# Moving GpSimd's arithmetic to VectorE in a hybrid RWKV-7, attention and MoE block, with preparation inputs issued a unit ahead

## The chip, the cores and the metric

One core of a Trainium2 chip. The metric is the device time of one launch in microseconds; a lower one is better. All tensors are float32 in HBM. Products that need float32 accuracy are made of three matmuls on the high and low parts of their operands (`mm3`): high by high, high by low, low by high. So most operands are split first: ScalarE copies the high part (`split`, L92), another engine subtracts it from the original to get the low part (L93).

## What is computed

A sequence of 2048 tokens of width 1024 goes through one layer:

```python
h = rms_norm(x, norm_mix_g)
u = h @ w_in
u_rwkv = centred_token_shift(u[..., :RWKV_COLS], mu_prev, mu_next)
...
y_rwkv = rwkv7_bidir(u_rwkv, ...)        # 8 heads of 64, forward and backward
y_attn = banded_gqa_attention(q, k, v)   # window of 128, blocks of 128
merged = sigmoid(gl_rwkv) * (y_rwkv @ w_proj_rwkv) + sigmoid(gl_attn) * (y_attn @ w_proj_attn)
x = x + merged @ w_out
x = x + expert_choice_moe(rms_norm(x, norm_ffn_g), w_router, w_gate, w_up, w_down)
return rms_norm(x, norm_final_g)
```

In the RWKV part the keys are scaled by `k_k` and normalized per head, decays and learning rates come from low-rank inputs, and the state runs over the tokens in both directions. In the expert part each of 16 experts takes the 256 tokens with the highest affinity.

## The kernel before

The kernel runs in stages, one after the other.

*First product.* `RwkvIn` computes the 15 channel blocks of `u_rwkv` (L78 to L80) and shifts them over the tokens; they go to HBM as `us`. Weights come through `w_load`, whose low part is GpSimd's unless another engine is named.

*Preparation.* `token_mixers` runs 32 units: 8 blocks of 256 tokens by 4 pairs of heads (`Prep`). `front()` computes decays (`th`, scans L289 and L290), `G`, `kd`, `KB` and `PR`; `back()`, called while the next unit's `front()` has been issued, makes the chunk matrices `A` (L328, L331), the bonus `bg` and transposed keys. Chunks have 32 tokens. Once per block `lora_in` loads the low-rank inputs and the key blocks, squares the keys, sums them per head on TensorE (L217), takes the reciprocal root by a chain of operations on 16 columns (`rsqrt`, L106 to L108), and transposes the result `rn` (L224). Between a unit's steps `between` issues five matmuls of `Proj` (`gates`, L459): these compute q, k, v and the gates, 2112 matmuls in all, as filling for TensorE. From the ninth unit on it also issues one step of an inversion (`Invert`, L386 and L387): a multiply of GpSimd and a sum of VectorE, 31 steps for each of three matrices here.

*Steps.* The state's chain goes over 64 chunks in both directions (L615 to L640); VectorE's multiply L636 carries the state from one chunk to the next. Around the chain, in an order that the program fixes, lie the other gate matmuls, the five other inversions, attention (L698 to L753) and the normalization of the RWKV output (`finish_rwkv`, L653 to L673).

*Mixer output.* Projections, the gated sum (`gl`, L953), the residual, the router's softmax (L1003 to L1009).

*Routing.* `route` finds each expert's threshold bit by bit: 30 rounds of a count (L1048), a sum over partitions by TensorE (L1051), and two operations of one column (L1052, L1053). GpSimd meanwhile makes `r5` and the low parts of the first three experts' weights.

*Experts.* 16 experts in 8 slices each; GpSimd only issues gathers and scatters there.

Each engine executes its queue in the order of the program that a scheduler has laid out; DMAs are issued by SP, ScalarE's queue and GpSimd's. The order around the change is set by the code: `issue_after(mark)` puts the gates behind a given instruction. The main loop reads:

```python
                if n < len(todo):
                    t0, p = todo[n]
                    if p == 2 and n + 4 < len(todo):
                        t1 = todo[n + 4][0]
                        lora[t1] = lora_in(k, t1, NT)
                    pp.append(Prep(k, t0, p, lora[t0], between))
                    pp[n].load()
                    pp[n].front()
                if n:
                    pp[n - 1].back()
```

## Time and profile before

| what | value |
|---|---|
| median of three runs | 3549.74 us (3541.02 to 3562.28) |
| the profiled execution | 3546.9 us, span 3545.0 us, mean granted clock of TensorE 0.944 |
| busy: TensorE, VectorE, ScalarE, GpSimd | 3201.6, 2288.4, 1447.1, 1018.3 us |
| stages (from 0): first product, transition, preparation | to 365, 400, 1035 us |
| steps, mixer output, routing, experts | to 1888, 2322, 2391, 3545 us |
| GpSimd in the experts | 180.0 us, gathers and scatters |

The stages are cut by the time of their first and last instructions. Between 1035 and 1052 us the last unit's matrices travel to the chain. A busy share is the time in which an engine executes, whatever slows it; an engine that waits for another counts as idle.

### The profile page before, as it was taken

The numbers are of one execution on the slowest core, as the hardware profiler recorded it, in microseconds if no ns is written. First come the engines' busy times: TensorE is split into PE (matmuls) and PEld (weight loads), VectorE is DVE, ScalarE is ACT, GpSimd is POOL, SyncE is SP. The second block draws the span as 40 slices with busy tenths as digits, with TensorE's granted clock in tenths as the row PEclk, the third lists the DMA queues.
The fourth block names the chain that finished last, engine by engine and source line by source line (L and its number), as shares of the span: only waits on it lengthen the run. The fifth ranks groups of instructions, "written<-read, shape, count | busy, mean of one in ns | idle before, by whom it ended". The sixth has DMA issues, their size and how long they took to land. (4 is left out here: it accounts for less than half of the span.)

```text
span 3545.0 us, 65905 instructions
## 1 busy us (share of the span) xinstructions
PE 3201.6 (90%) x26062; PEld 2620.6 (74%) x26062; DVE 2288.4 (65%) x4469; ACT 1447.1 (41%) x2679; POOL 1018.3 (29%) x1023
## 2 busy tenths in 40 slices
PE   7999687788778999899997999939999999999998
PEld 6888576666656556566665888829999999999997
DVE  7433467776777867976666555565666666666664
ACT  4111354544433444544543333214444444444443
POOL 3110245465743323233333222230211121112111
PEclk9999798899888999999998999959999999999999
DMA  4222576767678666667855555344766676667663
GB/s 145 92 75 86 158 208 178 212 193 205 180 215 203 160 151 165 183 164 194 199 152 198 196 196 189 137 171 157 258 238 224 227 257 241 221 227 258 240 221 132
DMA packets 464579, 665.19 MB, mean 188 GB/s; under 512 B 162312, under 2 KB 345480, under 8 KB 445968
## 3 DMA queue, kind: packets, MB, share of 16 engines
q1 hardware_dynamic: 387824, 535.14, 49.2%
q10 hardware_dynamic: 58304, 59.79, 5.3%
q0 software_dynamic: 18144, 66.07, 4.9%
q8 instruction: 205, 3.36, 0.4%
q14 instruction: 102, 0.84, 0.1%
HBM read 483.66 MB, written 177.21 MB: 186 GB/s over the span
## 5 line engine op out<-in xcount | busy, mean ns | idle before, releaser
L459 PE MATMUL mm<-h,w 128*128 128x512 f32 x2112 | 624.9, 429 | 18.8 <-ACT h L92 4.2
L86 PE MATMUL pg<-xs,wg 128*128 128x256 f32 x2048 | 583.8, 285 | 0.0
L87 PE MATMUL pg<-xs,wg 128*128 128x256 f32 x2048 | 582.5, 284 | 0.0
L88 PE MATMUL pg<-xs,wg 128*128 128x256 f32 x2048 | 580.0, 283 | 0.0
L459 PEld LDWEIGHTS mm<-h,w 128*128 128x128 f32 x2112 | 392.5, 199 | 116.5 <-issue 11.0
L87 PEld LDWEIGHTS pg<-xs,wg 128*128 128x128 f32 x2048 | 392.8, 192 | 4.6 <-DVE xs L1158 0.2
L86 PEld LDWEIGHTS pg<-xs,wg 128*128 128x128 f32 x2048 | 392.5, 192 | 4.6 <-ACT xs L1157 0.2
L88 PEld LDWEIGHTS pg<-xs,wg 128*128 128x128 f32 x2048 | 392.8, 192 | 0.0
L93 DVE TENSOR_TENSOR wg<-raw,wg 128x2048 fp32r<-128x2048 f32 x125 | 286.2, 2290 | 106.3 <-ACT wg L92 106.1
L93 POOL TENSOR_TENSOR w<-wraw,w 128x1024 fp32r<-128x1024 f32 x86 | 210.1, 2444 | 295.0 <-ACT w L92 251.7
L92 ACT ACTIVATE w<-wraw 128x1024 fp32r<-128x1024 f32 x135 | 142.5, 1057 | 273.3 <-issue 159.7
L92 ACT ACTIVATE wg<-raw 128x2048 fp32r<-128x2048 f32 x128 | 244.2, 1908 | 6.0 <-DMA raw<-w_exp 6.0
L1221 ACT ACTIVATE sg<-pg 128x256 f32<-128x256 f32 x128 | 49.3, 385 | 480.6 <-PE pg L88 458.6
L1147 POOL DMA_INDIRECT x<-z,idx x30 | 33.5, 1117 | 597.9 <-DVE z L1183 545.2
L627 ACT ACTIVATE W<-ps 32x128 f32<-32x128 f32 x512 | 137.2, 268 | 162.5 <-PE ps L622 145.6
L87 PE MATMUL py<-wd,hd 128*128 128x512 f32 x512 | 203.1, 397 | 0.0
L78 PE MATMUL mm<-h,w 128*128 128x512 f32 x480 | 188.9, 395 | 14.7 <-ACT w L92 12.2
L86 PE MATMUL py<-wd,hd 128*128 128x512 f32 x512 | 201.0, 393 | 0.0
L88 PE MATMUL py<-wd,hd 128*128 128x512 f32 x512 | 198.4, 390 | 0.0
L79 PE MATMUL mm<-h,w 128*128 128x512 f32 x480 | 188.6, 394 | 0.7 <-DVE h L126 0.7
L80 PE MATMUL mm<-h,w 128*128 128x512 f32 x480 | 188.2, 393 | 0.3 <-POOL w L93 0.3
L1222 DVE TENSOR_TENSOR sg<-pg,sg 128x256 f32<-128x256 f32 x128 | 54.0, 422 | 194.7 <-ACT sg L1221 194.7
(305 smaller groups left out, 7108.6 us busy)
## 6 DMA issues: line engine op xcount, KB each, us to landing
raw<-w_exp SPq DMA_DIRECT2D x128, 1536.0 KB, 6.9
wraw<-w_in SPq DMA_DIRECT2D x103, 512.0 KB, 4.5
PRA<-pra SPq DMA_DIRECT2D x64, 512.0 KB, 5.4
pra<-PR SPq DMA_DIRECT2D x64, 256.0 KB, 3.8
pra<-A SPq DMA_DIRECT2D x64, 256.0 KB, 3.7
kt<-KT ACTq DMA_DIRECT2D x128, 128.0 KB, 4.4
...
KT<-kt SPq DMA_DIRECT2D x128, 128.0 KB, 4.4
```

The costliest lines, as they stand in the source:

```text
L78: nc.tensor.matmul(ps, lhsT=w[:, 0, i], rhs=hs[i][:, 0], start=(i == 0), stop=False)
L79: nc.tensor.matmul(ps, lhsT=w[:, 0, i], rhs=hs[i][:, 1], start=False, stop=False)
L80: nc.tensor.matmul(ps, lhsT=w[:, 1, i], rhs=hs[i][:, 0], start=False, stop=(i == KD - 1))
L86: nc.tensor.matmul(out, lhsT=w[0], rhs=x[0], start=start, stop=False)
L87: nc.tensor.matmul(out, lhsT=w[0], rhs=x[1], start=False, stop=False)
L88: return nc.tensor.matmul(out, lhsT=w[1], rhs=x[0], start=False, stop=stop)
L92: nc.scalar.activation(hi, x, AF.Copy)
L93: (eng or nc.vector).tensor_sub(lo, x, hi)
L459: nc.tensor.matmul(self.ps, lhsT=w[:, t // 2, i], rhs=h[:, t % 2], start=(self.i == 0), stop=(self.i == 3 * KD - 1))
L627: nc.scalar.activation(W[qd(u), o, e].rearrange("p g i -> p (g i)"), ps[qd(u), 128:256], AF.Copy)
L1221: nc.scalar.activation(sg, pg[:, 0], AF.Silu)
L1222: nc.vector.tensor_mul(sg, pg[:, 1], sg)
```

## The change

GpSimd keeps its memsets, the copies of the identity that the chain needs, and indirect DMAs; its rows fall from 772 to 221 in the program. All other work is VectorE's or ScalarE's, or is left out. In the preparation, `PR` is made in four operations of 256 columns that read `G` from a buffer with one more column of ones per chunk, so the copies at the edges disappear. ScalarE takes the copies `gc`, the squares of the first stage, and the scale and bias of `yt`. `lora_in` becomes the class `LoraIn`, whose loads, products and norms are spread over the units of the block before; `krv` is loaded a unit ahead; the stores of `PR` stand at the start of `back()`. `Proj` loads raw weights ahead of their split, and 72 gate matmuls, not 24, stand at the beginning of the preparation. Of the 2112 gate matmuls 1178 stood ahead of the chain's first matmul and 1240 stand there now; the rest lie in the steps. In the routing, constants are loaded before the mixer output, and the low parts of the first three experts' weights are made by VectorE in 36 pieces of 256 columns, one for each bit where there are some left.

```diff
-BUFS = dict(all=3, th=2, ta=2, vt4=1, kk=2, A=2, KT=2, bg=2, krv=3, kd=2)
+BUFS = dict(all=3, th=2, ta=2, vt4=1, kk=2, A=2, KT=2, bg=2, kd=2, KB=2)
...
-    split(nc, w[:, 0], w[:, 1], raw, eng or nc.gpsimd)
+    split(nc, w[:, 0], w[:, 1], raw, eng)
...
-            if i % 2:
-                nc.gpsimd.tensor_mul(sq, x, x)
-            else:
-                nc.scalar.activation(sq, x, AF.Square)
...
+class LoraIn:
...
-            nc.gpsimd.tensor_sub(t[64:], raw[64:], t[64:])
...
+            nc.vector.tensor_sub(t[64:], raw[64:], t[64:])
...
+    def keys(self):
+        k, nc = self.k, self.k.nc
+        self.sq = []
+        for p in range(NPAIR):
+            sq = k.prep.tile([128, self.N], F32, name="sq", bufs=NPAIR)
+            nc.sync.dma_start(sq, k.us[:, 3 + 3 * p, self.sl])
+            self.sq.append(sq)
+
+    def squares(self):
+        for p in range(NPAIR):
+            self.k.nc.scalar.activation(self.sq[p], self.sq[p], AF.Square, scale=self.k.v("k_k", p))
+
+    def norms(self):
+        k, nc = self.k, self.k.nc
+        NJ = self.N // 128
+        ps = k.ps_l.tile([128, NJ, NPAIR, 2], F32, name="pl")
+        for p in range(NPAIR):
+            for j in range(NJ):
+                nc.tensor.matmul(ps[:, j, p], lhsT=self.sq[p][:, j * 128:(j + 1) * 128], rhs=k.bones2, start=True,
+                                 stop=True)
+        ss = k.prep.tile([128, 8 * NJ], F32, name="ss")
+        nc.vector.tensor_scalar(ss, ps.rearrange("p j q e -> p (j q e)"), 1e-24, None, op0=ALU.max)
+        self.rn = k.prep.tile([128, 8 * NJ], F32, name="rn", bufs=2)
+        rsqrt(k, k.prep, self.rn, ss)
+
+    def rows(self):
+        k, nc = self.k, self.k.nc
+        pt = k.ps_l.tile([8, self.N], F32, name="pl")
+        for j in range(self.N // 128):
+            nc.tensor.transpose(pt[:, j * 128:(j + 1) * 128], self.rn[:, j * 8:j * 8 + 8], k.ident)
+        self.rt = k.rts[self.t0 // self.N % 2]
+        nc.vector.tensor_copy(self.rt[0:8], pt)
...
-        G = tile("G", (2, NT))
-        nc.scalar.activation(G, th, AF.Exp, scale=-0.5 * DECAY)
+        G = k.G[self.t0 // NT * NPAIR + p & 1]
+        nc.scalar.activation(G[:, 0, :, 1:], cv(th)[:, 0], AF.Exp, scale=-0.5 * DECAY)
+        nc.scalar.activation(G[:, 1, :, :C], cv(th)[:, 1], AF.Exp, scale=-0.5 * DECAY)
...
-        nc.gpsimd.tensor_mul(kd, kd, both(kt))
+        nc.vector.tensor_mul(kd, kd, both(kt))
...
-        nc.gpsimd.tensor_mul(PR[:, :, :, 1], both(rt).rearrange("p d (c t) -> p d c t", t=C), cv(G))
...
-        ck, cG = kk.rearrange("p (c t) -> p c t", t=C), cv(G)
-        nc.vector.tensor_mul(PR[:, 0, :, 0, 1:], ck[:, :, 1:], cG[:, 0, :, :C - 1])
-        nc.vector.tensor_mul(PR[:, 1, :, 0, :C - 1], ck[:, :, :C - 1], cG[:, 1, :, 1:])
-        nc.gpsimd.tensor_copy(PR[:, 0, :, 0, 0:1], ck[:, :, 0:1])
-        nc.gpsimd.tensor_copy(PR[:, 1, :, 0, C - 1:], ck[:, :, C - 1:])
-        nc.gpsimd.tensor_copy(k.gc[:, 0, p, c0:c0 + NC], cG[:, 0, :, C - 1])
+        for d in range(2):
+            for x, t in ((0, kk), (1, rt)):
+                g0 = x if d == 0 else 1 - x
+                nc.vector.tensor_mul(PR[:, d, :, x], t.rearrange("p (c t) -> p c t", t=C), G[:, d, :, g0:g0 + C])
+        nc.scalar.activation(k.gc[:, 0, p, c0:c0 + NC], G[:, 0, :, C], AF.Copy)
...
-        nc.gpsimd.tensor_copy(k.gc[:, 1, p, lo:lo + NC][:, ::-1], cG[:, 1, :, 0])
-        for e in range(2):
-            nc.sync.dma_start(k.pra[self.q][half(e), :, p, e, self.ul].rearrange("r d c x -> r d (c x)"),
-                              PR[half(e)].rearrange("p d c x t -> p d (c x t)"))
+        nc.scalar.activation(k.gc[:, 1, p, lo:lo + NC][:, ::-1], G[:, 1, :, 0], AF.Copy)
...
+        for e in range(2):
+            nc.sync.dma_start(k.pra[self.q][half(e), :, p, e, self.ul].rearrange("r d c x -> r d (c x)"),
+                              PR[half(e)].rearrange("p d c x t -> p d (c x t)"))
...
-        nc.gpsimd.tensor_add(kd[:, 0], kd[:, 0], kd[:, 1])
-        nc.gpsimd.tensor_mul(kd[:, 1], rt, kd[:, 0])
+        nc.vector.tensor_add(kd[:, 0], kd[:, 0], kd[:, 1])
+        nc.vector.tensor_mul(kd[:, 1], rt, kd[:, 0])
...
-        nc.scalar.activation(bg[:, 0], bg[:, 0], AF.Identity, bias=k.v("ln_b", p))
...
-            (eng or nc.vector).tensor_mul(tmp[:, :i, :i], X[:, r, r], col[:, None, :].to_broadcast([128, i, i]))
+            nc.vector.tensor_mul(tmp[:, :i, :i], X[:, r, r], col[:, None, :].to_broadcast([128, i, i]))
...
+        for _ in range(2):
+            self.load()
...
+        n = self.loaded
+        if n < len(self.todo) + self.done:
+            k = self.k
+            raw = k.wpool.tile([128, KD, 128], F32, name="wraw", bufs=k.raw_bufs)
+            k.nc.sync.dma_start(raw, k.I["w_in"][self.order[n]])
+            self.raw.append(raw)
+            self.loaded += 1
+
+    def split(self):
+        if self.raw:
+            k = self.k
+            raw = self.raw.pop(0)
+            w = k.wpool.tile([128, 2, KD, 128], F32R, name="w")
+            split(k.nc, w[:, 0], w[:, 1], raw)
+            self.w.append(w)
...
-                    while len(self.w) < 2 and len(self.w) < len(self.todo):
-                        self.load()
+                    while len(self.w) < 2 and self.raw:
+                        self.split()
+                        if not self.done:
+                            self.load()
...
+                if self.i == KD and self.done:
+                    self.load()
...
-        nc.vector.scalar_tensor_tensor(out=yt[:, p].rearrange("c (k t) -> c k t", t=C), in0=pt[:, p],
-                                       scalar=k.v("ln_w", p), in1=bg[:, p, 0].rearrange("c (k t) -> c k t", t=C),
-                                       op0=ALU.mult, op1=ALU.add)
-    nc.gpsimd.tensor_mul(yt, yt, bg[:, :, 1])
+        nc.scalar.activation(yt[:, p].rearrange("c (k t) -> c k t", t=C), pt[:, p], AF.Identity,
+                             scale=k.v("ln_w", p), bias=k.v("ln_b", p))
+    nc.vector.tensor_add(yt, yt, bg[:, :, 0])
+    nc.vector.tensor_mul(yt, yt, bg[:, :, 1])
...
-    nc.gpsimd.tensor_sub(qs[64:], qr[64:], qs[64:])
+    nc.vector.tensor_sub(qs[64:], qr[64:], qs[64:])
...
-    nc.gpsimd.tensor_sub(kl[:, :, :W], kr[:, :, :W], kh[:, :, :W])
+    nc.vector.tensor_sub(kl[:, :, :W], kr[:, :, :W], kh[:, :, :W])
...
+            lora = {0: LoraIn(k, 0, NT)}
+            for i in range(3):
+                lora[0].load(i)
+            lora[0].keys()
...
+                    inv.run(1)
+
+            gates.run(GATE_FIRST)
+            ln = lora[0]
+            ln.squares()
+            ln.norms()
+            for i in range(3):
+                ln.make(i)
+            gates.run(GATE_FIRST)
+            ln.rows()
...
+                p = n % NPAIR
...
+                    t0 = todo[n][0]
+                    if n == 0:
+                        pp.append(Prep(k, t0, 0, lora[t0], between))
+                        pp[0].load()
+                    if n + NPAIR - p < len(todo):
+                        t1 = todo[n + NPAIR - p][0]
+                        if p == 0:
+                            lora[t1] = LoraIn(k, t1, NT)
+                        ln = lora[t1]
+                    else:
+                        ln = None
+                    if n + 1 < len(todo) and p < NPAIR - 1:
+                        pp.append(Prep(k, t0, p + 1, lora[t0], between))
+                        pp[n + 1].load()
+                    if ln:
+                        if p == 0:
+                            ln.load(1)
+                            ln.load(2)
+                        elif p == 1:
+                            ln.make(1)
+                            ln.keys()
+                            ln.load(0)
+                        elif p == 2:
+                            ln.make(2)
+                            ln.squares()
                     pp[n].front()
                 if n:
                     pp[n - 1].back()
+                if n < len(todo) and ln:
+                    if p == 2:
+                        ln.norms()
+                        ln.make(0)
+                    elif p == 3:
+                        ln.rows()
+                        pp.append(Prep(k, t1, 0, ln, between))
+                        pp[n + 1].load()
...
-        gates.eng = nc.gpsimd
...
-                nc.gpsimd.tensor_add(gl[:, 0], gl[:, 0], gl[:, 1])
+                nc.vector.tensor_add(gl[:, 0], gl[:, 0], gl[:, 1])
...
-                nc.vector.scalar_tensor_tensor(out=z, in0=x, scalar=rs, in1=gz, op0=ALU.mult, op1=ALU.mult)
+                with tc.issue_after(last):
+                    nc.vector.scalar_tensor_tensor(out=z, in0=x, scalar=rs, in1=gz, op0=ALU.mult, op1=ALU.mult)
...
+def route_constants(k, pool):
...
+    k.rc = [ld("same_e", 128), ld("less_e", 128), ld("rmask", 256), ld("iota", CAP + NBLK + 1)]
+    k.rc.append(pool.tile([128, 128], BF16, name="same_b"))
+    nc.vector.tensor_copy(k.rc[4], k.rc[0])
+    k.iota = pool.tile([128, CAP], BF16, name="iota_b")
+    nc.vector.tensor_copy(k.iota, k.rc[3][:, :CAP])
...
+        def part(a, i):
+            nc.vector.tensor_sub(rem, a, r5[:, :, :, i])
+            nc.scalar.activation(r5[:, :, :, i + 1], rem, AF.Copy)
+
+        rest = {27: lambda: part(k.aff, 2), 24: lambda: part(rem, 3)}
...
+            count = nc.vector.tensor_scalar(junk, aTf, cand.bitcast(F32)[:, 0:1], None, op0=ALU.is_ge, op1=ALU.add,
+                                            accum_out=cnt)
+            with tc.issue_after(count.ins):
+                if bit in rest:
+                    rest[bit]()
+                else:
+                    next(small, 0)
...
+        def first(raw):
+
+            wg = ws.tile([128, 2, 2, KD, 128], F32R, name="wg")
+            wd = ws.tile([128, 2, KD * 128], F32R, name="wd")
+            lo = []
+            for t, r in ((wg.rearrange("p s a i c -> p s (a i c)"), raw[:, 0:2].rearrange("p a i c -> p (a i c)")),
+                         (wd, raw[:, 2].rearrange("p a b -> p (a b)"))):
+                nc.scalar.activation(t[:, 0], r, AF.Copy)
+                lo += [(t, r, slice(j, j + 256)) for j in range(0, r.shape[1], 256)]
+            return (wg, wd), lo
+
+        def pieces(todo):
+            for t, r, sl in todo:
+                nc.vector.tensor_sub(t[:, 1, sl], r[:, sl], t[:, 0, sl])
+                yield 1
+
...
-            w = [weights(raws.pop(0), nc.gpsimd) for _ in range(3)]
+            w, lo = zip(*(first(raws.pop(0)) for _ in range(3)))
...
+        small = pieces([x for t in lo for x in t])
+        route(k, rp, small)
```

TensorE at the beginning of the preparation (`mm` are gates, `sq` squared keys, `rn` the norms, `lora,wup` the first unit's product), before:

```order
L459 MATMUL mm<-h,w 128x512 x24
L217 MATMUL pl<-bones_134,sq 128x2 x2
L279 MATMUL pt<-ident,krv 128x128 x2
L217 MATMUL pl<-bones_134,sq 128x2 x6
L224 MATMUL pl<-ident,rn 8x128 x2
L265 MATMUL pl<-lora_2387,wup 128x256
```

and now:

```order
L495 MATMUL mm<-h,w 128x512 x48
L469 MATMUL pt<-ident,ev 128x128 x4
L495 MATMUL mm<-h,w 128x512 x24
L235 MATMUL pl<-bones_134,sq 128x2 x8
L300 MATMUL pt<-ident,krv 128x128 x4
L246 MATMUL pl<-ident,rn 8x128 x2
L286 MATMUL pl<-lora_2490,wup 128x256
```

There are 72 gates where 24 stood, and the sums of squares and the transposition of `rn` follow them.

TensorE around the second block's norms, before:

```order
L217 MATMUL pl<-bones_134,sq 128x2 x2
L348 MATMUL pt<-ident,KB 128x128 x4
L459 MATMUL mm<-h,w 128x512
L217 MATMUL pl<-bones_134,sq 128x2 x2
L459 MATMUL mm<-h,w 128x512 x4
L279 MATMUL pt<-ident,krv 128x128 x2
L224 MATMUL pl<-ident,rn 8x128 x2
L265 MATMUL pl<-lora_2387,wup 128x256
```

In the changed order the sums stand here,

```order
L495 MATMUL mm<-h,w 128x512 x5
L367 MATMUL pt<-ident,KB 128x128 x4
L495 MATMUL mm<-h,w 128x512 x5
L235 MATMUL pl<-bones_134,sq 128x2 x8
L286 MATMUL pl<-lora_2490,wup 128x256
```

and the transposition of `rn` here, 27 rows further on:

```order
L495 MATMUL mm<-h,w 128x512 x5
L367 MATMUL pt<-ident,KB 128x128 x4
L495 MATMUL mm<-h,w 128x512 x5
L246 MATMUL pl<-ident,rn 8x128 x2
L286 MATMUL pl<-lora_2654,wup 128x256
```

A unit's matmuls and gates lie between them now; the transposition was right behind the sums and a handful of gates.

VectorE at the start of the routing (`aff` the affinities, `aT` their transposition, `junk` the count, `wg,wd` experts' weights), before:

```order
L995 SCALAR_TENSOR_TENSOR z<-x_22686,rs_22761,gz 128x1024
L1008 RECIPROCAL sms<-sms 128x1
L1009 TENSOR_SCALAR aff<-sme,sms 128x16
L1038 COPY aT<-pr 128x256
L1048 TENSOR_SCALAR junk,cnt<-aT,cand 128x256
L1052 TENSOR_SCALAR mi<-pr 128x1
L1053 SCALAR_TENSOR_TENSOR cand<-mi,cand 128x1
L1048 TENSOR_SCALAR junk,cnt<-aT,cand 128x256
L1052 TENSOR_SCALAR mi<-pr 128x1
```

and now:

```order
L1090 TENSOR_SCALAR aff<-sme,sms 128x16
L1076 SCALAR_TENSOR_TENSOR z<-x_22657,rs_22732,gz 128x1024
L1294 TENSOR_TENSOR wg<-raw,wg 128x256 x4
L1294 TENSOR_TENSOR wd<-raw,wd 128x256 x4
L1123 COPY aT<-pr 128x256
L1129 MEMSET cand 128x1
L1142 TENSOR_SCALAR junk,cnt<-aT,cand 128x256
L1294 TENSOR_TENSOR wg<-raw,wg 128x256
L1151 TENSOR_SCALAR mi<-pr 128x1
L1152 SCALAR_TENSOR_TENSOR cand<-mi,cand 128x1
L1142 TENSOR_SCALAR junk,cnt<-aT,cand 128x256
```

`z` stands behind `aff`; eight pieces of weights stand ahead of the loop and one in each round behind the count.

## Rows read from the trace of the kernel before

**Rows 1.** Stage, its us; busy us of PE, PEld, DVE, ACT, POOL; clock; DMA.
```profile
0.00:365.00 365.00, 345.39 (x1519) 285.00 (x1520) 178.88 (x215) 82.04 (x84) 63.71 (x67) 0.99 0.29 98
365.00:400.00 35.00, 7.06 (x29) 5.67 (x27) 13.22 (x26) 9.31 (x19) 7.81 (x9) 0.58 0.62 187
400.00:537.00 137.00, 121.33 (x958) 99.77 (x958) 87.33 (x138) 70.71 (x135) 57.38 (x69) 0.91 0.69 195
537.00:1035.00 498.00, 397.19 (x3142) 315.48 (x3140) 349.83 (x514) 228.38 (x442) 280.18 (x304) 0.89 0.68 198
...
1052.00:1888.00 836.00, 765.83 (x9966) 500.39 (x9966) 625.03 (x1493) 386.90 (x1138) 266.78 (x350) 0.94 0.68 171
1888.00:2322.00 434.00, 403.41 (x1926) 333.33 (x1927) 243.66 (x511) 141.42 (x216) 125.23 (x69) 0.97 0.55 188
2322.00:2391.00 69.00, 13.60 (x84) 9.31 (x85) 48.84 (x165) 10.15 (x9) 28.35 (x15) 0.50 0.47 172
```

**Rows 2.** What TensorE waited for in the preparation: total us, times, longest.
```profile
PE pl L224 <- DVE rn L108: 37.3, 8, 8.9
PE pt L328 <- DVE KB L303: 17.8, 7, 4.1
```

**Rows 3.** Groups of the preparation: busy us, mean ns | idle before, releasers.
```profile
L386 POOL TENSOR_TENSOR tmp<-X,N 128x1 f32<-128x1 f32 (+30 forms) x93 | 109.1, 1173 | 57.0 <-DVE X L387 30.5 <-DMA N<-pra 11.2 <-DVE rsq_t L107 8.3
...
L93 DVE TENSOR_TENSOR w<-wraw,w 128x1024 fp32r<-128x1024 f32 x46 | 72.3, 1574 | 28.1 <-ACT w L92 28.0
L296 POOL TENSOR_TENSOR kd<-kd,krv 128x512 f32<-128x512 f32 x32 | 49.8, 1558 | 113.6 <-ACT kd L295 113.4
...
L290 DVE TENSOR_TENSOR_SCAN th<-smask,th 128x256 f32<-128x256 f32 x32 | 38.0, 1189 | 0.0
...
L305 DVE TENSOR_TENSOR PR<-kk,G 128x248 f32<-128x248 f32 x32 | 30.6, 955 | 0.3 <-ACT G L292 0.2
```

**Rows 4.** Single lines over the whole run: duration in ns, minimum/median/maximum.
```profile
L290 DVE TENSOR_TENSOR_SCAN th<-smask,th x32: 658/668/3080, 403.8 to 1002.8; 128x256 f32<-128x256 f32 x32
L297 DVE SCALAR_TENSOR_TENSOR ta<-ta,kk x32: 659/762/1781, 407.8 to 1005.8; 128x512 f32<-128x512 f32 x32
L305 DVE TENSOR_TENSOR PR<-kk,G x32: 383/1050/1934, 409.2 to 1006.4; 128x248 f32<-128x248 f32 x32
L93 DVE TENSOR_TENSOR w<-wraw,w x49: 1207/1225/3372, 341.4 to 1033.2; 128x1024 fp32r<-128x1024 f32 x49
L386 DVE TENSOR_TENSOR tmp<-X,N x155: 150/668/3159, 1042.0 to 1498.8; 128x1 f32<-128x1 f32 x5, 128x4 f32<-128x4 f32 x5, 128x9 f32<-128x9 f32 x5, 128x16 f32<-128x16 f32 x5
```

**Rows 5.** TensorE's waits in the transition, 365 to 400 us.
```profile
PE pl L217 <- ACT sq L215: 21.9, 3, 17.2
```

**Rows 6.** Groups of the steps, 1052 to 1888 us, as rows 3.
```profile
L386 DVE TENSOR_TENSOR tmp<-X,N 128x289 f32<-128x289 f32 (+30 forms) x139 | 133.4, 960 | 7.8 <-DMA kr<-kT 4.3 <-DMA N<-pra 0.7
...
L93 POOL TENSOR_TENSOR w<-wraw,w 128x1024 fp32r<-128x1024 f32 x39 | 95.6, 2452 | 132.6 <-ACT w L92 89.3 <-PE pa L710 18.7 <-ACT W L627 14.0
```

**Rows 7.** TensorE's wait for VectorE's state multiply (steps), and that multiply's group.
```profile
PE ps L615 <- DVE W L636: 20.7, 17, 3.3
...
L636 DVE TENSOR_TENSOR W<-ps,gc 64x256 f32<-64x256 f32 x252 | 106.0, 420 | 90.3 <-PE ps L633 81.2 <-ACT ur L619 5.1 <-ACT W L627 1.4
```

**Rows 8.** L733 of the attention, as rows 4.
```profile
L733 DVE TENSOR_SCALAR sc<-sc,den x128: 339/413/2589, 1118.4 to 1871.6; 128x384 f32<-128x384 f32 x112, 128x256 f32<-128x256 f32 x16
```

**Rows 9.** Routing's timeline (start, duration, engine, instruction), then L1053 as rows 4.
```profile
2325.41 0.48 DVE L1048 TENSOR_SCALAR_CACHE_REDUCE junk<-aT,cand 128x256 f32<-128x256 f32 x1
...
2326.51 4.52 POOL L93 TENSOR_TENSOR wg<-raw,wg 128x2048 fp32r<-128x2048 f32 x1 [0.18 <-ACT wg L92]
2326.54 0.48 DVE L1048 TENSOR_SCALAR_CACHE_REDUCE junk<-aT,cand 128x256 f32<-128x256 f32 x1
...
2327.48 3.57 DVE L1053 SCALAR_TENSOR_TENSOR cand<-mi,cand 128x1 int32<-128x1 int32 x1
...
L1053 DVE SCALAR_TENSOR_TENSOR cand<-mi,cand x30: 158/160/3569, 2323.7 to 2370.5; 128x1 int32<-128x1 int32 x30
```

130 lines of the change are left out of this document (51 added, 79 removed).

## The prediction

> **What bounds the kernel now.** I read the stages first, then, stage by stage, what TensorE waited for, then the groups, then single durations. The profiled execution took 3546.9 us, 2.8 us under the median of the three runs (3549.74); the sum is made against it. The table of stages [rows 1] shows TensorE busy for most of every stage but three: the transition 365-400 us (7.06 of 35), the preparation's last six blocks 537-1035 us (397 of 498, granted clock 0.89), and the routing 2322-2391 us (13.6 of 69). The experts, from 2391 us on, are TensorE's and the change leaves them alone. So time can come from those three stages, and a little from the steps (766 of 836) and the mixer's output (403 of 434).
>
> In the six blocks VectorE is busy for 350 of 498 us, but that figure hides something. A scan of 256 columns takes 658 ns at its shortest and 3080 at its longest [rows 4], and averages 1189 in the preparation [rows 3]; L305, with 248 columns, takes 383 to 1934 and averages 955; the weight split takes 1207 to 3372 and averages 1574. The rows of the routing show how: while GpSimd ran a subtraction of 4.52 us, VectorE's L1053, one element wide, took 3.57 us; its median over 30 is 0.16 [rows 9]. **VectorE stands still while GpSimd does arithmetic**, and GpSimd has 280 us of work in those 498 us. From the shortest durations the stretch of these three groups alone is 72.3 - 46x1.207 = 16.8, 38.0 - 32x0.658 = 16.9, 30.6 - 32x0.383 = 18.3: 52 us [rows 3, 4]. Five more groups per unit (the other scan, three operations of 512 columns, the other of 248) are of the same shapes; at about 8 us each (half of these, since L297's median of 762 is near its minimum) I estimate 90 us in all.
>
> **The change, part by part.** *Preparation (400-1035).* VectorE receives, at undisturbed lengths: kd's multiply, 512 columns like L297, 32 x 0.66 = 21; PR in four operations of 256 columns instead of two of 248, so 64 more at 0.39 (L305) = 25; kd's add and multiply, 64 x 0.39 = 25; the low-rank subtractions, some 15 at 0.66 = 10; the inversion's 93 multiplies, at the median of the same line on VectorE (0.668) 62, at its mean in the steps (0.960, partly stretched) 89 [rows 4, 6]: I take 83, nearer the mean since the sizes are uneven. Together 164. It loses the 90 of stretch. VectorE's total goes from 87 + 350 = 437 to about 511 us; TensorE's is 121 + 397 = 518 at clocks of 0.91 and 0.89, less at full clock. In the six blocks: 350 + 83 + 6/8 x 81 - 6/8 x 90 = 426, so 71 us a block for VectorE against 66 for TensorE and 83 now. A unit's chain still crosses engines, so I put the block at 77, halfway between 71 and 83: -36. The first two blocks lose their share of the norm wait: -9. The norms account for much of both: TensorE waits 37.3 us in 8 waits for rn, and 17.8 for KB [rows 2], which GpSimd's kd (1558 ns a piece) feeds. With norms a unit ahead the 37.3 goes; what is late next is KB and A, now behind more work on VectorE. Sum **-45**, ends -81 (TensorE and VectorE never waiting) and -9. The loads issued ahead and the PR stores moved behind them are SP's; what queues behind the later stores is the inversion's load N, which today costs GpSimd 11.2 us of idle [rows 3], whose idle cost nothing; VectorE's queue would hold everything behind it, so 0 if the load is early enough, 11 at worst, which I keep in the end at -9; I take 0, since the first step of an inversion stands a unit behind its last store. ScalarE gets G in halves and gc; at 228 of 498 us it covers them.
>
> *Transition.* All key blocks load at once instead of two at a time, and 48 more gate matmuls fill it. TensorE's three waits for squares sum to 21.9, the longest 17.2 [rows 5]; the other two, 4.7, are the second pairs and go. The first shortens by what the keys stood behind; it cannot go entirely, since the last shifted channel must land first. I take **-9**, between -4.7 and -12.
>
> *Steps (1052-1888).* The 62 gate matmuls that no longer lie here (1240 before the first chain step, 1178 now, of 2112) cost 345.39/1519 = 0.227 us each [rows 1]: -14. VectorE gets 39 weight splits [rows 6], 16 subtractions of qs as wide at 1.22 too, and 16 of kl with 768 columns at 1.22 x 0.75 = 0.92: 82 us. The yt operations cancel against the scale that ScalarE takes. It loses stretch: L386 133.4 - 139 x 0.668 = 40, L733 with 413 ns median and 2589 at most [rows 6, 8], and the rest by estimate, 80 in all. So VectorE stays near 625 of 836 us, in shorter pieces than 3 us. TensorE's waits for its state multiply, 20.7 in 17 [rows 7], halve: -10. **-25**, ends +25 (the waits double and nothing else gives) and -70 (TensorE alone, 752).
>
> *Mixer output.* The weight splits and additions move onto a VectorE that is busy 244 of 434: **-5**, 0 to -8, from its end, where a chain of small operations is stretched today.
>
> *Routing.* A bit takes 2326.54 - 2325.41 = 1.13 us undisturbed [rows 9]; 30 bits would take 34; from the first L1053 to the last now are 46.9 us for 29 of them. But each bit gets one 256-column subtraction (0.39) that only partly fits the wait for the count, so 1.33 us a bit, 40 in all: -7. Against that, eight pieces stand in front of the loop, 8 x 0.41 = 3.3, behind ScalarE's high parts, which wait for the weights: +5. **-2**, ends -6 and +6.
>
> *First product (0-365).* GpSimd's 16 squares go to ScalarE (82 of 365 busy), 15 splits to VectorE (179 of 365): 0, ends -3 and +5.
>
> Sum: -45 - 9 - 25 - 5 - 2 = -86, so **3461 us**.
>
> [...] GpSimd keeps its memsets of W between chain steps, 240 of them. One-input operations like L733 are stretched today up to 2589 ns [rows 8]. [...]
>
> **Rivals.**
> (a) *VectorE bounds the preparation at today's pace.* Its chain per unit grows by 4 operations in line; 83 us a block stays. For: 426 us of work in six blocks is more than the 350 of now. Against: 71 a block. 3461 + 36 = **3497**.
> (b) *Memsets go on stretching one-input operations.* Then I estimate that a quarter of the steps' 80 us of stretch stays, and at worst all of it on the path: 3461 + 20 = **3481**. For: L733's longest is 2589 ns. Against: a memset writes 256 columns on 32 partitions, a subtraction here takes 2452 ns [rows 6], which is what the longest L733 looks like.
> (c) *The norms are not ahead in effect*: rn's chain of 1-16-column operations queues behind VectorE's own work and TensorE still waits 30 of 37.3: **3491**. The order of TensorE's rows speaks against it: a unit stands between.
> (d) *Everything runs at TensorE's or VectorE's pace*: blocks at 71 us (-72 -9), steps -70: 3546.9 - 81 - 9 - 70 - 5 - 2 = **3380**.
> (e) *Slower.* The 71 subtractions moved to VectorE in the steps each wait for ScalarE's high part at the head of an in-order queue, with the state multiply behind them. If each costs the chain its 1.22 us: 87; if also a wait as long as GpSimd's now, 89.3/39 = 2.3 us [rows 6]: 250. The rest gives -75 (-45 -9 -14 -5 -2). It decides from 93/71 = 1.31 us a piece, where the sum passes +18; at 1.75, 124 - 75 = +49: **3596**. Against: ahead of the state multiply VectorE idles 81.2 us for TensorE [rows 7], so there are gaps for 82 us of work, and TensorE waits only 17 times.
>
> **How the numbers follow.** Measured changes under 0.5% (17.7 us) can hardly be told from none. Chances: forecast (3415-3495) 0.50, (a) 0.18, (b) 0.08, (c) 0.05, (d) 0.12, (e) 0.07. Faster is all of them but (e) and the tail of (a) and of the forecast where the steps give +25: 0.87; same 0.08; slower 0.05 (part of (e) falls short of +18). The range leaves out (e) and the lower part of (d): 3395 to 3530.
>
> **What would show it.** GpSimd's total falls from 1018 us to under 400; no VectorE operation of one element above 0.5 us in the routing, scans near 0.66 us; TensorE's wait for rn gone (else c); preparation's blocks at 77 us with VectorE near 90% (83: a); the wait for the state multiply near 10 us (60 and more: e); the transition 26 us; the first expert matmul some 86 us earlier, the experts' length unchanged at 1154 us. If the experts change length, or the gain lies in the steps and not in the preparation, the argument was wrong.

## The result and the profile after

The changed kernel took 3437.24 us (median of four runs, 3432.75 to 3449.03) against 3553.57 us for the kernel before (four runs, 3541.02 to 3562.28): a ratio of 0.968, 95% interval 0.9641 to 0.972. The forecast was 3461, so the gain was 116 us where 89 (to the median then shown) was expected. The profiled execution took 3432.75 us, with a span of 3430.9 and a mean granted clock of 0.962. GpSimd executed 457 instructions in it where it was 1023, and was busy for 285.5 us where it was 1018.3.

The stages of the changed kernel, cut at events that both kernels have; the columns are those of [rows 1], whose cuts are a few us away from these. The lines are, in order: first product, transition, the whole preparation up to the first chain matmul, steps up to the last state multiply, the rest up to the last affinity, routing, experts.

```profile
0.00:364.50 364.50, 342.77 (x1504) 283.74 (x1505) 175.83 (x228) 86.24 (x98) 2.15 (x34) 0.98 0.27 97
364.50:400.20 35.70, 22.41 (x100) 17.94 (x99) 20.75 (x37) 13.50 (x21) 3.31 (x7) 0.79 0.81 244
...
400.20:968.70 568.50, 505.10 (x4148) 401.59 (x4147) 472.67 (x952) 295.56 (x650) 13.08 (x26) 0.96 0.77 227
...
968.70:1751.50 782.80, 731.28 (x9758) 485.22 (x9758) 595.96 (x1468) 388.80 (x1147) 84.83 (x265) 0.96 0.69 176
1751.50:2207.50 456.00, 417.54 (x2075) 341.89 (x2071) 275.64 (x636) 158.99 (x270) 0.00 (x0) 0.96 0.56 187
2207.50:2277.40 69.90, 14.09 (x86) 9.54 (x86) 47.02 (x208) 12.70 (x12) 3.97 (x4) 0.50 0.45 167
2277.40:3430.90 1153.50, 1136.85 (x8401) 1063.29 (x8400) 733.41 (x1377) 514.44 (x632) 178.15 (x122) 0.99 0.62 223
```

The same stretch of the kernel before, from its first unit to its first chain matmul:

```profile
400.20:1052.70 652.50, 528.35 (x4142) 422.83 (x4141) 446.74 (x685) 302.77 (x582) 347.11 (x397) 0.89 0.69 198
```

Where the 114 us of span went:

| stage (events) | before | after | difference | forecast |
|---|---|---|---|---|
| first product, to its last matmul | 361.6 | 364.5 | +2.9 | 0 |
| transition, to the first unit | 38.7 | 35.7 | -3.0 | -9 |
| preparation, to the first chain matmul | 652.4 | 568.5 | -83.9 | -45 |
| steps, to the last state multiply | 817.3 | 782.8 | -34.5 | -25 |
| to the last affinity | 451.6 | 456.0 | +4.4 | -5 |
| routing, to the first expert matmul | 69.7 | 69.8 | +0.1 | -2 |
| experts | 1153.7 | 1153.6 | -0.1 | 0 |

In the preparation TensorE ran the same matmuls in 505.1 us instead of 528.4 (its clock rose from 0.89 to 0.96) and was idle for 63.4 us instead of 124.1. What it still waited for there, as [rows 2]:

```profile
PE pl L246 <- DVE rn L108: 8.4, 3, 4.4
PE mm L495 <- DVE h L93: 6.8, 5, 2.8
PE mm L495 <- DVE w L93: 6.8, 5, 4.0
PE pt L348 <- DVE rn L108: 6.5, 1, 6.5
```

TensorE waited 14.9 us for rn, 8.4 at its transposition (L246) and 6.5 at L348, where it waited 37.3 us at the transposition before. VectorE's groups of that stage, as [rows 3], without GpSimd beside them:

```profile
L405 DVE TENSOR_TENSOR tmp<-X,N 128x1 f32<-128x1 f32 (+30 forms) x107 | 75.2, 702 | 24.1 <-DMA kt<-KT 8.2 <-DMA N<-pra 8.0 <-DMA pra<-PR 4.5
L93 DVE TENSOR_TENSOR w<-wraw,w 128x1024 fp32r<-128x1024 f32 x48 | 58.6, 1223 | 24.6 <-ACT w L92 24.6
...
L328 DVE TENSOR_TENSOR PR<-krv,G 128x256 f32<-128x256 f32 x64 | 26.2, 419 | 0.3 <-ACT G L314 0.3
...
L310 DVE TENSOR_TENSOR_SCAN th<-smask,th 128x256 f32<-128x256 f32 x32 | 21.9, 685 | 3.7 <-ACT th L309 3.6
...
L318 DVE TENSOR_TENSOR kd<-kd,krv 128x512 f32<-128x512 f32 x32 | 21.8, 680 | 2.0 <-ACT kd L317 2.0
```

These means are now near the shortest durations of before [rows 4]: the weight split 1223 ns (its mean was 1574), a scan 685 (up to 1189). kd's multiply takes 680 ns here and took GpSimd 1558.

The routing's difference of nothing hides two changes. This is its start on the timeline (start, duration, engine, instruction; in brackets the idle time before it and what ended it):

```profile
2207.55 0.23 DVE L1090 TENSOR_SCALAR aff<-sme,sms 128x16 f32<-128x16 f32 x1
...
2216.84 1.91 ACT L1288 ACTIVATE wg<-raw 128x2048 fp32r<-128x2048 f32 x1 [2.12 <-DMA raw<-w_exp]
2218.08 1.28 DVE L1076 SCALAR_TENSOR_TENSOR z<-x,rs,gz 128x1024 f32<-128x1024 f32 x1 [10.30 <-DMA out<-z]
2218.66 1.04 ACT L1288 ACTIVATE wd<-raw 128x1024 fp32r<-128x1024 f32 x1
2219.28 1.42 DVE L1294 TENSOR_TENSOR wg<-raw,wg 128x256 fp32r<-128x256 f32 x4
2220.62 1.43 DVE L1294 TENSOR_TENSOR wd<-raw,wd 128x256 fp32r<-128x256 f32 x4
2222.25 0.42 DVE L1123 COPY aT<-pr 128x256 f32<-128x256 f32 x1 [0.20 <-DMA out<-z]
```

The counts of the loop (durations, first and last start):

```profile
L1142 DVE TENSOR_SCALAR_CACHE_REDUCE junk<-aT,cand x30: 479/479/479, 2222.7 to 2255.7; 128x256 f32<-128x256 f32 x30
```

The loop's first count comes 15.2 us after the last affinity; before, it came 1.3 us after. From the first count to the last the loop takes 33.0 us, where it took 46.9 (first to last L1053 in [rows 9]). The 256-column pieces, one a round, fit entirely into the wait for the count: a round takes 33.0/29 = 1.14 us with them and took 1.13 without [rows 9]. The `raw` loads of 1536 KB are slices, not experts: the 36 pieces are those of the first expert's first three slices.

### The profile page after: what moved, and what is told of

It reads as the page before. It is cut to its first block, busy times and chain, and to the rows that moved or that the text cites. A ratio compares the mean times of both kernels' runs of the same rounds, so it can differ in the third digit from the quotient of the medians.

```text
span 3430.9 us, 65672 instructions
## 1 busy us (share of the span) xinstructions
PE 3170.0 (92%) x26062; PEld 2603.2 (76%) x26062; DVE 2321.3 (68%) x4902; ACT 1470.2 (43%) x2828; POOL 285.5 (8%) x457
## 5 line engine op out<-in xcount | busy, mean ns | idle before, releaser
L495 PE MATMUL mm<-h,w 128*128 128x512 f32 x2112 | 602.1, 419 | 28.7 <-ACT ev L519 7.5
L495 PEld LDWEIGHTS mm<-h,w 128*128 128x128 f32 x2112 | 383.2, 194 | 123.0 <-DVE w L93 9.8
L405 DVE TENSOR_TENSOR tmp<-X,N 128x1 f32<-128x1 f32 (+30 forms) x248 | 188.4, 760 | 37.9 <-DMA N<-pra 17.6
L78 PE MATMUL mm<-h,w 128*128 128x512 f32 x480 | 190.0, 397 | 18.5 <-ACT w L92 12.8
L93 DVE TENSOR_TENSOR w<-wraw,w 128x1024 fp32r<-128x1024 f32 x135 | 164.8, 1222 | 50.4 <-ACT w L92 50.0
L79 PE MATMUL mm<-h,w 128*128 128x512 f32 x480 | 189.3, 395 | 0.0
L80 PE MATMUL mm<-h,w 128*128 128x512 f32 x480 | 188.8, 394 | 0.0
```

The source lines that it names most:

```text
L78: nc.tensor.matmul(ps, lhsT=w[:, 0, i], rhs=hs[i][:, 0], start=(i == 0), stop=False)
L79: nc.tensor.matmul(ps, lhsT=w[:, 0, i], rhs=hs[i][:, 1], start=False, stop=False)
L80: nc.tensor.matmul(ps, lhsT=w[:, 1, i], rhs=hs[i][:, 0], start=False, stop=(i == KD - 1))
L93: (eng or nc.vector).tensor_sub(lo, x, hi)
L405: nc.vector.tensor_mul(tmp[:, :i, :i], X[:, r, r], col[:, None, :].to_broadcast([128, i, i]))
L495: nc.tensor.matmul(self.ps, lhsT=w[:, t // 2, i], rhs=h[:, t % 2], start=(self.i == 0), stop=(self.i == 3 * KD - 1))
```

## The experiments

All are edits of the changed kernel, and stage times below are from one profiled execution each. Kernels with the same code in a stage show how far such times scatter: the preparation gave 566.4 to 569.1 us in six of them, the steps up to the last state multiply 778.9 to 787.6.

**Does GpSimd's work alone slow VectorE?** Work on which nothing depends is added to GpSimd in the preparation.

```diff
                 gates.run(GATE_PREP, after=mark)
+                with tc.issue_after(mark):
+                    nc.gpsimd.tensor_mul(dm, pp[min(n, 31)].krv[:, 0:2], pp[min(n, 31)].krv[:, 1:3])
```

> The changed kernel plus, at each of a unit's seven steps, a GpSimd multiply of 128x512 that reads the unit's loads and writes a tile nobody reads: about 290 us of GpSimd arithmetic in the preparation, on which nothing depends. Theory (VectorE stands still while GpSimd does arithmetic): VectorE's busy time in the preparation rises from 472 us by 80 to 110, its scans' mean from 0.68 to over 1 us, and the preparation from 568 us (first unit to first chain matmul) to 630 to 660. Rival (the gain came from no longer waiting for GpSimd's results and from the loads and norms ahead): VectorE's durations and the preparation stay within 5 us.

The total was 3590.78 us, slower than the kernel before. The stage from first unit to first chain matmul:

```profile
404.20:1126.30 722.10, 550.13 (x4148) 431.58 (x4146) 637.02 (x950) 296.79 (x647) 358.74 (x242) 0.87 0.62 178
```

Three groups in it:

```profile
L892 POOL TENSOR_TENSOR dm<-krv 128x512 f32<-128x512 f32 x217 | 346.5, 1597 | 330.9 <-DMA krv<-us 316.3
...
L319 DVE SCALAR_TENSOR_TENSOR ta<-ta,kk 128x512 f32<-128x512 f32 x32 | 39.1, 1223 | 0.0
L351 DVE TENSOR_TENSOR A<-pt,amask 128x512 f32<-128x512 f32 x64 | 43.5, 681 | 12.1 <-PE pt L348 8.6 <-DMA wraw<-w_in 3.4
```

VectorE is busy 164 us longer (637.0 against 472.7) for the same instructions, and the preparation 154 us: the theory holds, and the price is higher than was expected. Operations with two operands in SBUF are stretched (L319: 1223 ns against 685); L351, which reads one operand from PSUM, is not (681 against 684). TensorE's longest waits in the stage are all for VectorE (27.4 us for w's low part at L495, 19.8 and 19.4 for bg), none for the loads that GpSimd now reads too. The clock fell from 0.96 to 0.87.

**Does GpSimd work that reads nothing do the same?** The multiply is replaced by memsets.

```diff
+                with tc.issue_after(mark):
+                    nc.gpsimd.tensor_copy(dm[:, 0, :1], pp[min(n, 31)].krv[:, 0, :1])
+                    for _ in range(3):
+                        nc.gpsimd.memset(dm, 1.0)
```

> As the run with GpSimd multiplies, but with three memsets of 128x512 in the place of each multiply (and a copy of one column): about as many microseconds of GpSimd, which read nothing from SBUF. Theory from the multiplies' run (VectorE stands still whenever GpSimd works): the preparation rises to 680 to 720 us, VectorE's scans to over 1 us. Rival (only GpSimd operations that read SBUF hold VectorE's operations with two inputs): scans stay near 0.68 us and the preparation within 15 us of 568.

The total was 3438.98 us and the preparation 567.8 us. Two groups of it:

```profile
L894 POOL MEMSET dm<- 128x512 f32 x663 | 348.7, 526 | 38.3
...
L319 DVE SCALAR_TENSOR_TENSOR ta<-ta,kk 128x512 f32<-128x512 f32 x32 | 22.0, 686 | 0.0
```

The rival of the expectation came: VectorE is busy for 475.0 us, 2.3 more than in the changed kernel, and its operations with two inputs are not stretched (L319: 686 ns against 685). But the memsets do hold L101, an operation of 16 columns with one input, here in the preparation of the changed kernel and then of this one (durations in ns, minimum/median/maximum):

```profile
L101 DVE TENSOR_SCALAR rn<-rn x7: 166/171/176, 437.5 to 850.9; 128x16 int32<-128x16 int32 x7
```

```profile
L101 DVE TENSOR_SCALAR rn<-rn x7: 158/328/551, 436.0 to 849.2; 128x16 int32<-128x16 int32 x7
```

A memset takes 526 ns here. L406, a sum over columns with one input, is not held: it averages 464 ns beside the memsets and 465 without. In all VectorE's busy time is only the 2.3 us above longer. What sets L101 apart from L406 no run shows, and whether it is the reading or the arithmetic of a multiply that holds the two-input operations, no run tells apart.

For rival (b) the hold of L101 means that its mechanism is there and its price is not. With the 240 memsets of W still in the steps, L733 of [rows 8], now L772, never takes more than 553 ns. Of its 128 instances the six that overlap a memset take 414 to 553 ns, the others at most 432.

```profile
L772 DVE TENSOR_SCALAR sc<-sc,den x128: 344/415/553, 1048.6 to 1788.0; 128x384 f32<-128x384 f32 x112, 128x256 f32<-128x256 f32 x16
```

**How much of the preparation's 84 us is which part?** Two parts are undone, one at a time and both together. GpSimd back:

```diff
-        nc.vector.tensor_mul(kd, kd, both(kt))
+        nc.gpsimd.tensor_mul(kd, kd, both(kt))
...
-                nc.vector.tensor_mul(PR[:, d, :, x],
+                (nc.gpsimd if x else nc.vector).tensor_mul(PR[:, d, :, x],
...
-        nc.vector.tensor_add(kd[:, 0], kd[:, 0], kd[:, 1])
-        nc.vector.tensor_mul(kd[:, 1], rt, kd[:, 0])
+        nc.gpsimd.tensor_add(kd[:, 0], kd[:, 0], kd[:, 1])
+        nc.gpsimd.tensor_mul(kd[:, 1], rt, kd[:, 0])
...
-                    inv.run(1)
+                    inv.run(1, nc.gpsimd)
```

> The changed kernel with kd's multiply, PR's r half, kd's add and multiply and the inversions' multiplies in the preparation back on GpSimd; everything ahead stays ahead. It takes 140 us of work from VectorE and, at the stretch of the idle multiplies (164 us for 358 us of GpSimd), gives it back 120. Theory (taking the work off GpSimd gave most of the 84 us): the preparation goes from 568 to 620 us or more. Rival (issuing ahead gave most): it stays under 590.

Nothing ahead (instead of the loads, products and norms spread over the block before):

```diff
+                    if p == 2 and n + 2 < len(todo):
+                        t1 = todo[n + 2][0]
+                        ln = lora[t1] = LoraIn(k, t1, NT)
+                        for i in (1, 2, 0):
+                            ln.load(i)
+                            ln.make(i)
+                        ln.keys()
+                        ln.squares()
+                        ln.norms()
+                        ln.rows()
+                    if n:
+                        pp.append(Prep(k, t0, p, lora[t0], between))
+                        pp[n].load()
                     pp[n].front()
```

> The changed kernel with GpSimd's work on VectorE, but the low-rank inputs, keys, squares and norms in one piece before the third unit of each block, and krv loaded by its own unit, as in the kernel before. Theory (taking the work off GpSimd gave most): the preparation stays under 590 us. Rival (issuing ahead gave most): TensorE waits for rn again, 30 us or more, and the preparation is 605 us or longer.

On TensorE this does not bring back the norms' place of before. From the second block on, the transposition of rn stood 0 to 12 matmuls behind the last sum of squares before and stands 118 to 186 behind it in the changed kernel; with nothing ahead it is still 76 to 108, and 76 to 89 with both undone.

Both:

> Both undone in the preparation: GpSimd has its arithmetic again and nothing is issued ahead. One alone gave 615.8 and 584.4 us against 568.5. If the two are independent: 568.5 + 47.3 + 15.9 = 632 us. If the norms' chain suffers from GpSimd's work more than the sum says (its operations of 16 columns are held for whole GpSimd instructions): 645 to 655 us, as before's 652.

The preparation's line of each, in the order GpSimd back, nothing ahead, both:

```profile
399.40:1015.20 615.80, 526.54 (x4148) 415.83 (x4146) 439.69 (x697) 294.39 (x650) 298.41 (x279) 0.92 0.73 210
```

```profile
399.80:984.20 584.40, 517.74 (x4148) 415.54 (x4146) 475.63 (x954) 297.95 (x654) 12.48 (x26) 0.93 0.76 222
```

```profile
400.10:1024.20 624.10, 531.97 (x4148) 425.10 (x4147) 451.35 (x700) 299.06 (x654) 296.15 (x279) 0.90 0.72 208
```

GpSimd's work costs 47.3 us, just short of the theory's 620 us for the stage, and not going ahead 15.9; together they cost 55.6, less than the sum of 63.2 and clear of the 645 that a held norm chain was to give. In the run with nothing ahead TensorE waits 11.8 us for KB at L322, and only 1.9 us for rn at its transposition; with both undone it is 0.5 us for rn. So the 37.3 us of [rows 2] did not come back, and what the norms' place was worth is not measured by these runs. From 624.1 to the 652.4 of before 28 us are left, for the distance between the sums and the transposition, the edge copies, the copies of gc, the low-rank subtractions on GpSimd, the stores of PR and the gates at the start; these were not tried apart. The totals of the three were 3455.35, 3430.85 and 3462.84 us. The second is under the changed kernel's, though its preparation is 16 us longer; that is taken up below.

**Did GpSimd cost time in the steps?**

```diff
-    nc.vector.tensor_sub(qs[64:], qr[64:], qs[64:])
+    nc.gpsimd.tensor_sub(qs[64:], qr[64:], qs[64:])
...
-    nc.vector.tensor_mul(yt, yt, bg[:, :, 1])
+    nc.gpsimd.tensor_mul(yt, yt, bg[:, :, 1])
...
         k.ps_gate.pop()
+        gates.eng = nc.gpsimd
```

kl's subtraction goes back in the same way, and `gates.eng` is the engine of the weights' low parts from there on.

> The changed kernel with the weight splits, attention's subtractions and the last multiply of yt back on GpSimd from the steps on (the preparation unchanged). Theory (VectorE's standing still behind GpSimd made TensorE wait in the steps): from the first chain matmul to the last state multiply 800 to 810 us instead of 783, TensorE's wait for the state multiply 15 us or more instead of 5, the clock at half speed for 90 us or more instead of 65. Rival (the 62 gate matmuls fewer gave it, 14 us): 780 to 788.

The total was 3458.24 us; from the first chain matmul to the last state multiply 821.1 us passed, 38 more than in the changed kernel, and TensorE waited:

```profile
PE ps L655 <- DVE W L676: 22.8, 15, 3.6
```

In the changed kernel the same wait was 5.2 us; before it was 20.7 [rows 7]. The mean granted clock of the stretch was 0.94 instead of 0.96. The theory's direction holds, and the time is above its range. How much of the 38 us is GpSimd's work is open: this version has 14 more gate matmuls in the steps and another order of attention's matmuls (below), and up to the last affinity it is only 27 us longer than the changed kernel.

**Were the gates ahead worth 0.227 us each?**

```diff
-            gates.run(GATE_FIRST)
             ln = lora[0]
...
-            gates.run(GATE_FIRST)
             ln.rows()
```

> The changed kernel with 24 gate matmuls at the beginning of the preparation instead of 72. Theory (the transition is set by loads and the norm chain, the 48 matmuls lie in a hole and save 48 x 0.227 = 11 us later): the transition stays at 34 to 37 us, the steps and the mixer's output take 9 to 13 us more. Rival (the gates lengthen the transition by what they save): transition 25 to 28 us and the same total.

Neither came in full. The total was 3390.66 us, 47 less than the changed kernel's median. The transition was 31.4 us, 4.3 less, the preparation 561.0, and from the first chain matmul to the last affinity 1208.6 us passed with 48 more gate matmuls in them, against 1238.8. Something else in the steps had moved.

**What moved in the steps.** The order of TensorE's rows shows where to look: in the changed kernel 40 of attention's 808 matmuls (L748, L749, L780, L787) start behind the chain's last output product (L679). Other versions, though most change nothing in the steps' code, have another number there:

| version | behind the last L679 | first chain matmul to last affinity, us |
|---|---|---|
| before | 2 | 1268.9 |
| changed | 40 | 1238.8 |
| nothing ahead | 28 | 1224.1 |
| GpSimd back in the preparation | 13 | 1215.6 |
| both | 13 | 1215.9 |
| one gate chunk first | 10 | 1208.6 |
| routing and start (below) | 13 | 1211.1 |
| GpSimd back in the steps | 2 | 1266.0 |
| the six others | 40 | 1237 to 1244 |

When attention ends against the chain, in the changed kernel and then in the last version below (durations, first and last start):

```profile
L787 PE MATMUL pa<-pT,vs x184: 592/595/1116, 1057.8 to 1796.2; 128*64 128x512 f32 x184
...
L679 PE MATMUL y<-W,PRA x2048: 219/219/317, 981.8 to 1760.8; 128*32 128x64 f32 x187
```

```profile
L787 PE MATMUL pa<-pT,vs x184: 592/595/1061, 1043.4 to 1741.4; 128*64 128x512 f32 x184
...
L679 PE MATMUL y<-W,PRA x2048: 219/219/316, 973.8 to 1737.7; 128*32 128x64 f32 x187
```

In the changed kernel attention trails the chain by 35 us, in the other by 4. Where GpSimd is out of the steps, the fewer of attention's matmuls trail, the shorter the stretch, by up to 30 us. That the order is the cause is argued from this table; no run changed the order alone. The trailing end by itself is not the whole of it, as the same stretch shows in the changed kernel and in the last version (columns as [rows 1]):

```profile
968.70:2207.50 1238.80, 1148.83 (x11829) 827.11 (x11829) 871.60 (x2103) 547.79 (x1417) 84.83 (x265) 0.96 0.64 180
```

```profile
960.30:2171.30 1211.00, 1132.07 (x11829) 812.99 (x11829) 877.90 (x2105) 547.64 (x1417) 84.94 (x265) 0.97 0.66 185
```

Of the 28 us between them 17 are a shorter busy time of TensorE for as many matmuls, and 11 are idle time. Why is open. It follows that an edit's price cannot be read from these totals, only from stages whose order it leaves alone. The 14 us for 62 gates are not seen either: with 48 of them back in the steps these were 2.5 us shorter than in the last version, which has all of them ahead and 13 trailing matmuls to their 10. As the orders differ, this does not disprove them.

**What holds the routing's start?** First z got a second buffer, then the pieces a later place, then both.

```diff
-                z = xp.tile([128, D], F32, name="z")
+                z = xp.tile([128, D], F32, name="z", bufs=2)
```

> The changed kernel with a second buffer for z. In the changed kernel 69.9 us pass from the last affinity to the experts' first matmul; VectorE stands idle 10.3 us of them before z, whose only buffer waits for the store of the tile before. Theory: z is not what ends the wait, since the eight pieces behind it need the third expert's weights, whose high part ends at 12.2 us after the affinity; so the stretch stays at 68 to 70 us and the total at 3437. Rival: the buffer is the cause; then the loop starts about 10 us earlier, the stretch is 60 us.

```diff
-        for _ in small:
-            pass
+        with tc.issue_after(k.placed.ins):
+            for _ in small:
+                pass
```

`k.placed` is the copy into `pos`, the routing's last step on VectorE.

> The changed kernel with the last eight pieces of weights placed behind the routing's last step on VectorE, z with one buffer as it was. Theory: z alone still waits until about 11 us after the affinity, so only the 2.9 us of the pieces go: stretch 67 us. Rival (pieces alone are the cause): 58 us.

> Both edits. Theory: the two waits stand one behind the other and each alone hides the other; with both gone the loop starts about 1.5 us after the affinity instead of 14.9: stretch 57 us, total near 3425. Rival: the experts' weights or the gathers end the stretch, then it stays at 65 to 70 us.

The stretch from the last affinity to the first expert matmul was 67.8, 72.2 and 70.9 us, the totals 3434.01, 3432.61 and 3434.70. The first came to within 0.2 us; the second and the third failed. The timeline of the kernel with both edits shows a third wait:

```profile
2208.48 0.23 DVE L1090 TENSOR_SCALAR aff<-sme,sms 128x16 f32<-128x16 f32 x1
2208.62 1.28 DVE L1076 SCALAR_TENSOR_TENSOR z<-x,rs,gz 128x1024 f32<-128x1024 f32 x1
...
2209.93 0.34 SPq L1077 DMA_DIRECT2D out<-z  x1
2220.94 0.42 DVE L1123 COPY aT<-pr 128x256 f32<-128x256 f32 x1 [11.04 <-DMA out<-z]
```

z is ready at once, and then `aT` waits 11 us for z's store: it lies where the mixer output's buffers were. All three waits lead back to the same loads. Three loads of expert weights, one slice each, are issued 6 to 8 us ahead of the last affinity; the pieces need the third, and the last two of z's stores land 14.7 and 10.8 us after their issue, where the store ahead of the loads took 2.9. The same kernel's transfers from 2185 to 2224 us (count, KB each, median from issue to landing):

```profile
raw<-w_exp SPq DMA_DIRECT2D x3, 1536.0 KB, 6.5
x<-x SPq DMA_DIRECT2D x3, 512.0 KB, 3.5
out<-z SPq DMA_DIRECT2D x3, 512.0 KB, 10.8
```

To take all three waits away:

```diff
-                z = xp.tile([128, D], F32, name="z")
+                z = xg if b == ORDER[-1] and tt == 3 else xp.tile([128, D], F32, name="z")
...
-        aT = tp.tile([128, 2, 128], F32, name="aT")
+        aT, junk, cand, mi, cnt = k.early
```

`k.early` are tiles of the pool of routing constants, and the code puts the eight pieces behind the first slice's gate matmuls.

> Three waits were found to end within 3 us of each other at the routing's start: z for the store before it, the eight pieces for the third expert's weights, and aT, whose memory is that of z, for z's own store. Here all three are taken away: the last z is written into xg, aT and the loop's small tiles get memory of their own ahead of the mixer output, and the eight pieces stand behind the first slice's gate matmuls. Theory (the stores lie behind 4.5 MB of weights in the queues, and these three alone hold the loop): the loop starts 1.5 to 3 us after the last affinity instead of 15.2, and the experts' first matmul comes 55 to 59 us after it instead of 69.8; total 3419 to 3425. Rival (the gathers or the weights end the stretch): 65 to 70 us, total within 5 us of 3433.

The loop starts 1.8 us after the affinity and the stretch is 60.0 us, 1 us over the range; the total 3421.09 lies in it. The loop itself, to the end of its last count, lasted 37.2 us instead of 33.4: one of its rounds took 4.21 us where 1.13 is usual, the next 1.93. In the long round VectorE's timeline shows the eight pieces, which were meant to stand behind the first slice's gate matmuls:

```profile
2219.46 1.43 DVE L1293 TENSOR_TENSOR wg<-raw,wg 128x256 fp32r<-128x256 f32 x4 [0.21 <-ACT wg L1287]
2220.81 0.15 DVE L1150 TENSOR_SCALAR mi<-pr 128x1 int32<-128x1 f32 x1
2220.88 1.42 DVE L1293 TENSOR_TENSOR wd<-raw,wd 128x256 fp32r<-128x256 f32 x4
2222.21 0.15 DVE L1151 SCALAR_TENSOR_TENSOR cand<-mi,cand 128x1 int32<-128x1 int32 x1
```

They ran as soon as the third slice's high part was there, between the steps of one round, and a step of r5 followed them. So the edit moved the loop's start and took the pieces into the loop. The last version moves the two steps of r5, and keeps the next block's low-rank products out of the first rn chain (in the changed kernel they sat in it: the chain's operation at 396.09 us was followed at 398.81, after a wait for ScalarE).

```diff
-        rest = {27: lambda: part(k.aff, 2), 24: lambda: part(rem, 3)}
+        rest = {12: lambda: part(k.aff, 2), 8: lambda: part(rem, 3)}
...
-                            ln.make(1)
+                            with tc.issue_after(lora[t0].done.ins):
+                                ln.make(1)
```

The same is done for the two other products; `done` is the copy into `rt`.

> The version with the routing's three waits taken away, and two more edits: the two steps that finish r5 at the bits 12 and 8 instead of 27 and 24 (there the loop waited 4 us behind ScalarE's copies of weights that had not landed), and the next block's low-rank products behind the first block's rn (one of them stood in rn's chain on VectorE and waited for ScalarE). Theory: the loop takes 33.4 us instead of 37.2, the stretch from the last affinity to the first expert matmul 56 us instead of 60.0, the transition 33 us instead of 35.7; total 3412 to 3420, 0.5 to 0.7% under the changed kernel. Rival: the gathers or the third slice's weights take it back, total 3420 to 3435.

It took 3386.9 us (median of five, 3381.19 to 3392.68), 0.9542 of before with a 95% interval of 0.9518 to 0.9566, more than expected. The loop did not: it took 35.8 us and not 33.4, since the eight pieces still ran in one of its rounds, of 3.68 us, and the stretch was 58.7 us instead of 56. Routing gave 11 us, the transition 3.7 (32.0 us), the preparation 4. The other 28 us lie between the first chain matmul and the last affinity (1211.1 us against 1238.8), where this version edits nothing: the order again, as far as the table shows. It beats both kernels, but half of its gain over the changed one came with an order that nobody aimed at.

## Why the prediction was right, and where its steps failed

The time lies in the range, 24 us under the forecast. By span the preparation gave 39 us more than its term, the transition 6 less, the first product 3 and the routing 2 less; the steps and the mixer output together met theirs.

*VectorE stands still while GpSimd does arithmetic.* Right for operations with two SBUF inputs under GpSimd's multiplies, and shown by the idle multiplies (L319: 1223 ns against 685); under memsets L319 kept its 686 ns, and of the operations with one input L101 took up to 551 ns, where 176 was the most without, and L772 up to 553 beside the memsets of W, where 432 was. The stretch was sized from shortest durations, and those were nearly met.

*Preparation, -45.* The mechanism was right, the size was not: -83.9, past the lower end given (-81). The step that failed is "I put the block at 77, halfway between 71 and 83". From the first use of the third block's rn to the last `A` the six blocks took 428.0 us, 71.3 each.

```profile
519.30:947.30 428.00, 372.33 (x3114) 294.38 (x3113) 373.59 (x735) 218.08 (x481) 3.35 (x6) 0.95 0.77 227
```

VectorE's need in them was also set too high: 426 us forecast, 373.6 measured, 62 a block. The inversion's 93 multiplies took 70.9 us where 83 had been put down. The stretch that went away was some 86 us in these blocks where 6/8 of 90 had been put down, an estimate from the groups' means before and after. TensorE needed 372.3 us, not 397, mostly because its clock rose from 0.89 to 0.95 (397.2 x 0.89/0.95 = 372.1). The text named the clock and then priced nothing for it: 23 us of the 84 are the same matmuls run faster. The first two blocks gave 17.7 us instead of 9.

*Norms.* The text let the 37.3 us go; 14.9 us of waits for rn were left. GpSimd's work was worth 47 us of the stage alone. Undoing the look-ahead cost 16 us, but on TensorE it left the transposition far behind the sums, so whether the text gave the norms too much weight is open.

*Transition, -9.* Only -3.0, and with the first product's +2.9 the first unit starts at the same 400.2 us. The text took the 48 more gates as filling; with 24 the transition was 4.3 us shorter, so in part they lengthened it. rn's chain ended no earlier than before, since a low-rank product of the next block stood in it. Most of the first product's +2.9 is the row below: ScalarE's squares, which were costed at nothing, hold TensorE for 4.1 us where the same wait was 1.5.

```profile
PE mm L78 <- ACT sq L131: 4.1, 1, 4.1
```

*Steps, -25, and mixer output, -5.* Together -30.1, as forecast, but by luck. The waits for the state multiply fell by 15.5 us instead of 10; the 14 us for fewer gates were not found. Putting GpSimd back cost 38 us in the steps and 27 up to the last affinity, and 50 to 57 against the versions with 10 or 13 trailing matmuls, so the order that came with the change may have given back up to 30 us. How the -30.1 splits is open. The 40 us of stretch in L386 came from setting a median against a mean of uneven sizes; by the means of this line before and now, 960 and 803 ns, it was 22.

*Routing, -2.* The result +0.1 was near, as two errors cancelled. The loop gained 13.9 us instead of 7, as the pieces, one a round, cost nothing; its start lost 13.9 instead of 5. The text saw the wait for the weights and missed the stores' two waits.

*Rivals.* (a) and (c) did not come: blocks at 71 us, 14.9 us for rn where (c) had 30. (b)'s mechanism is there, as a memset lengthens L772 from at most 432 to at most 553 ns, but six such overlaps are far from 20 us. (d) came true in the preparation and not in the steps. (e) did not come: the 71 subtractions left a wait of 5.2 us behind the state multiply.
